# Hybrid short-conv and conformer block: tiles 3 and 4 of the FFN's input turned by VectorE and DRAM instead of TensorE

## The chip, the cores and the metric

The kernel runs on one core of one Trainium2 chip. The metric is device time in microseconds of one launch; of the kernel before three runs are shown. Besides, one execution was taken by the hardware profiler; views of that trace are quoted in fences. Engines are named as the profile names them: PE is TensorE (PEld its weight loads), DVE VectorE, ACT ScalarE, POOL GpSimd, SP SyncE, which here only issues DMAs (SPq). L659 is line 659 of the kernel.

## What is computed

One decoder block over 1024 tokens of width 1024, in float32, with 16 learned tokens ahead that are dropped at the end:

```
mix = mixer(rms_norm(h, pre_mix_norm), ...)       # input projection, two gated convolution groups, w_out
h   = h + rms_norm(mix, post_mix_norm)
xn  = rms_norm(h, pre_ffn_norm)
ff  = (silu(xn @ w_gate) * (xn @ w_up)) @ w_down
out = h + rms_norm(ff, post_ffn_norm)
```

The change lies between the mixer's output projection and the first gate and up products. There, token-major rows of `h` are normalised (`xn`) and have to be turned, so that the model dimension lies on partitions and they can be the moving operand of the gate and up products.

## The kernel before

**Precision.** Every product runs as three float32r matmuls, high x high, high x low and low x high (`mm3`, L105 to 109). For every operand ScalarE makes the high part (a cast) and VectorE the low part (a subtraction).

**Output projection in product groups.** The 1024 tokens are eight tiles of 128. `group` (L858) computes the output projection of three, three and two tiles: (0, 1, 2), (3, 4, 5), (6, 7). In a group the loop runs over the eight blocks k of the contraction; before each of the first six k the function given for that step in `at` is traced, and `at[6]` ahead of the last two. Everything stands under a manual schedule, so each engine, and each engine's DMA queue, runs its instructions in the order in which this Python code issues them. At the end of a group `leave_psum` (L617) empties the PSUM banks: ScalarE squares, VectorE multiplies by the gain gB_post.

**Norms.** `norms` (L633) takes a group's tiles: it forms the first inverse root, adds the residual rows (`hs`, loaded by `residual_x`, L628), writes `h` to DRAM (hd), squares, forms the second inverse root, and scales with gB_ffn into the tiles hn0 to hn7 (L651). `between` and `first` are pieces of other work traced inside it.

**Turning.** There are two ways. `turn` (L654) gives a tile to TensorE: eight 128x128 transposes into two PSUM banks, which ScalarE copies to the raw blocks (and, for tile 3, also casts and VectorE subtracts for B11). The other way takes tiles 0, 1 and 2: `send` (L668) lets VectorE transpose 32x32 blocks (STREAM_TRANSPOSE) and writes the tile to DRAM (xd); `fetch` (L672) reads it back with four DMAs so that the blocks come to their places; `receive` (L677) casts and copies into the raw blocks and B11. All of these DMAs, the weight loads and the residual rows go through SP's queue.

**Blocks.** raw[q, b] holds half q of the model dimension for tiles 4b to 4b+3. B11 is raw[0, 0] as high and low parts, B21 is raw[1, 0]. The gate and up products run in pairs of weight blocks by a Strassen-like scheme with seven products each (`Pair`, L723); the first two products, of pairs 0 and 1, read B11, all four tiles of it. The next two read B21, and T2 (sums of raw blocks, `t1_sum`, `t2_sum`, L915 to 930) comes after them.

**Where the pieces stood.** Group (6, 7) had tile 3's turn ahead of its sixth k (`b21`, L972, with B21's casts), and the turns of tiles 4 and 5, B11's last parts for T1 and the first operands ahead of its last two k (`early`, L978). Tiles 3, 4 and 5 were normalised before the group's code began.

**Buffers.** Two pools matter. `wp` has three buffers for each of the tags ws, wh, wl (raw weights, high and low parts). `tp` has five buffers of one tag, "t", and takes the two gains gB_post and gB_ffn (until the norms of the last group), the tiles hn, and some of the gate and up weights:

```
tp = ctx.enter_context(tc.tile_pool(name="tp", bufs=5))                              # L64
n[i] = row(tp, "t", f"hn{i}", TT)[:, :D]                                             # L644, in norms
if i == 1 or ((m, j % 2) == (0, 0) if j > 1 else (m, j) == (1, 1)):                  # L736, in Pair.load
    t = row(tp, "t", f"u{j}{m}{i}", TT)[:, :D]
else:
    t = wp.tile([P, D], F32, tag="ws", name=f"u{j}{m}{i}")
```

A buffer is given to a new tile when all that read or write the old one, by the program, have done so; the first instruction that writes the new tile waits for that. The pool `rp`, four buffers of 8 KB a partition, holds half of the projection's moving data and, as those are used up, B21; the transposed tiles on their way to DRAM go there after the change.

Of the kernel before, what the change touches and what calls it, by code (L numbers as in the profile page):

```python
# [8 lines left out]
F32 = mybir.dt.float32  # L9
# [45 lines left out]
def hybrid_block(ctx: ExitStack, tc: tile.TileContext, xT, x, w_first, w_in, w_out, w_gate, w_up, w_down, par, g_post, g_ffn, g_out, out):  # L55
# [39 lines left out]
    def big(name, dt=F32R, pool=None):  # L95

        return (pool or xg).tile([P, 4 * HALF], dt, tag="x", name=name)
# [56 lines left out]
        nc.sync.dma_start(raw_w["o", k], w_out[k])  # L154

    def split_o(k, eng=None):
        if k in (3, 4):
            wu[k] = [held[k - 3][:, q, :] for q in range(2)]
        else:
            wu[k] = [wp.tile([P, D], F32R, tag=t, name=f"{t}_o{k}") for t in ("wh", "wl")]  # L160
        nc.scalar.copy(wu[k][0], raw_w["o", k])
        (eng or nc.vector).tensor_tensor(wu[k][1], raw_w["o", k], wu[k][0].bitcast(F32), op=ALU.subtract)

    def third(j):
# [463 lines left out]
    def residual_x(i):  # L628
        h = hp.tile([P, D], F32, tag="h", name=f"h{i}")
        nc.sync.dma_start(h, x[i * P : (i + 1) * P, :])  # L630
        return h

    def norms(grp, left, s1, hs, between=None, first=None):  # L633
        n_ = len(grp)
        v = sm.tile([P, 16], F32, tag="s2", name=f"pm{grp[0]}")
        nc.vector.tensor_tensor(v[:, :n_], s1[:, 0:n_], s1[:, 4 : 4 + n_], op=ALU.add)
        r = rsqrt_n(v[:, :n_], 1.0 / D, RMS_EPS, n_, f"pm{grp[0]}")
        if first:
            first()
        v2 = sm.tile([P, 16], F32, tag="s2", name=f"pf{grp[0]}")  # L640
        n = {}
        for q, i in enumerate(grp):
            nc.vector.scalar_tensor_tensor(hs[i], left[i], r[:, q : q + 1], hs[i], op0=ALU.mult, op1=ALU.add)
            n[i] = row(tp, "t", f"hn{i}", TT)[:, :D]  # L644
            nc.scalar.activation(n[i], hs[i], AF.Square, accum_out=v2[:, q : q + 1])
            nc.sync.dma_start(hd[i], hs[i])
        if between:
            between()
        r = rsqrt_n(v2[:, :n_], 1.0 / D, RMS_EPS, n_, f"pf{grp[0]}")
        for q, i in enumerate(grp):  # L650
            nc.vector.scalar_tensor_tensor(n[i], hs[i], r[:, q : q + 1], gB["ffn"], op0=ALU.mult, op1=ALU.mult)  # L651
        return n

    def turn(i, n, at=(0, 1)):  # L654
        c = slice((i % 4) * P, (i % 4 + 1) * P)
        for q in range(2):
            pt = bank(at[q], f"pt{i}_{q}")
            for k in range(4):
                nc.tensor.transpose(pt[:, k * P : (k + 1) * P], n[:, (4 * q + k) * P : (4 * q + k + 1) * P], ident)  # L659
            p4 = pt.rearrange("p (a b) -> p a b", a=4)  # L660
            nc.scalar.copy(raw[q, i // 4][:, :, c], p4)
            if (q, i // 4) == (0, 0):
                nc.scalar.copy(B11[0][:, :, c], p4)
                nc.vector.tensor_tensor(B11[1][:, :, c], p4, B11[0][:, :, c].bitcast(F32), op=ALU.subtract)

    xd = {i: dram.tile([P, D], F32, tag=f"xd{i}", name=f"xd{i}") for i in range(3)}

    def send(i, n, t):  # L668
        nc.vector.transpose(t.rearrange("p (j k q) -> p j k q", j=4, k=8), n.rearrange("p (k j q) -> p j k q", k=8, j=4))
        nc.sync.dma_start(xd[i], t)  # L670

    def fetch(i, n):  # L672
        for j in range(4):
            src = xd[i].rearrange("(i r) (j x) -> j r i x", i=4, j=4)[j]
            nc.sync.dma_start(n[32 * j : 32 * j + 32].rearrange("r (i x) -> r i x", i=4), src)

    def receive(i, n):  # L677
        c = slice(i * P, (i + 1) * P)
        split4 = lambda t: t[:, :, c].rearrange("p k (i q) -> p k i q", i=4)
        for q in range(2):  # L680
            n4 = n.rearrange("p (i k q) -> p k i q", i=4, k=8)[:, 4 * q : 4 * q + 4]
            if q == 0:
                nc.scalar.copy(split4(B11[0]), n4)
                nc.vector.tensor_tensor(split4(B11[1]), n4, split4(B11[0]).bitcast(F32), op=ALU.subtract)
            nc.scalar.copy(split4(raw[q, 0]), n4)

    st = None
    free = [5, 6, 7, 4, 0, 1, 2, 3]
# [34 lines left out]
    class Pair:  # L723
# [19 lines left out]
        def a_side(self, n, m):  # L743
            a11, a12 = self.u[m, 0][:, :512], self.u[m, 0][:, 512:]
            if n not in (1, 2):
                a21, a22 = self.u[m, 1][:, :512], self.u[m, 1][:, 512:]
            if n == 1:
                s = a11
            elif n == 6:
                add(a21, a21, a22)  # L750
                sub(a11, a21, a11)
                s = a11
            elif n == 2:
                s = a12
            elif n == 5:
                s = a21
            elif n == 7:
                sub(a21, a22, a11)
                s = a21
            elif n == 3:  # L760
                sub(a12, a12, a11)
                s = a12
            else:
                s = a22
            return s
# [92 lines left out]
    def group(grp, ks, at):  # L858
        pm = {i: [bank(b, f"po{i}{q}") for q, b in enumerate(OUT_BANKS[j])] for j, i in enumerate(grp)}

        def mm(i, k):
            c = slice(i * P, (i + 1) * P)
            for q in range(2):
                d = slice(q * 512, (q + 1) * 512)
                mm3(pm[i][q], yh[k][:, c], yl[k][:, c], wu[k][0][:, d], wu[k][1][:, d], k == ks[0], k == ks[-1])

        for s, k in enumerate(ks[:-2]):
            at.get(s, lambda: None)()
            for i in grp:
                mm(i, k)  # L870
        at.get(6, lambda: None)()
        for i in grp:
            for k in ks[-2:]:
                mm(i, k)
        s1 = sm.tile([P, 16], F32, tag="s1", name=f"s1_{grp[0]}")
        return s1, {i: leave_psum(i, pm[i], s1, q) for q, i in enumerate(grp)}

    def ahead(k=None, n=None):

        def f():  # L880
            if k is not None:
                split_o(k)
            if n is not None:
                load_o(n)

        return f
# [13 lines left out]
        fetch(i, hn[i])  # L900

    def turns(*grp, at=(0, 1)):
        return lambda: [turn(i, hn.pop(i), at if q else (0, 1)) for q, i in enumerate(grp)]

    def back(i):
        return lambda: receive(i, hn.pop(i))

    hs = {i: residual_x(i) for i in (3, 4, 5)}
    s1, left = group((3, 4, 5), middle, {1: ahead(0, 5), 2: ahead(1, 6), 3: lambda: [ahead(2, 7)(), back(0)()], 4: back(1), 5: back(2)})
    hn = norms((3, 4, 5), left, s1, hs)  # L910

    n_hi = [0]
    X = {1: B11}

    def t1_sum(i):  # L915
        c = slice(i * P, (i + 1) * P)
        r11, r12 = raw[0, 0], raw[0, 1]
        sub(r11[:, :, c], r12[:, :, c], r11[:, :, c])
# [13 lines left out]
    def split_lo(o, src):  # L932
        for h in range(2):
            s = slice(2 * h, 2 * h + 2)
            sub(o[1][:, s, :], src[:, s, :], o[0][:, s, :].bitcast(F32))
# [4 lines left out]
    def copy_hi(o, src):  # L940
        for h in range(2):
            s = slice(2 * h, 2 * h + 2)
            nc.scalar.copy(o[0][:, s, :], src[:, s, :])
# [6 lines left out]
    def a_high(s, *places):  # L950
        if s >= len(order) or s in made:
            return
        j, n = order[s]
        if j > 1 and n == 1 and j + 1 < NP:
            pairs[j + 1] = Pair(j + 1)
        src = sums.pop(s, None) or [pairs[j].a_side(n, m) for m in range(2)]
        made[s] = [operand_hi(src[m], f"{n}_{j}{m}", places[m] if places else None) for m in range(2)]
        high[s] = src
# [6 lines left out]
        a_high(s, *places)  # L965
        a_low(s)

    def pairs_load():
        split_o(7)
        pairs[1].load(0, (0,))  # L970

    def b21():  # L972
        turns(3)()
        X[2] = pair("B21", (rp, rp))
        copy_hi(X[2], raw[1, 0])
        split_lo(X[2], raw[1, 0])

    def early():  # L978
        for q in range(2):
            raw[q, 1] = blocks(big(f"raw{q}1", F32))  # L980
        turns(4, 5, at=(5, 6))()
        pairs[1].load(0, (1,))
        for i in range(2):
            t1_sum(i)
        a_side(0)
        a_side(1, (hp, "h"), (jp, "jk"))

    hs = {i: residual_x(i) for i in (6, 7)}
    s1, left = group((6, 7), up, {1: ahead(5), 2: lambda: [split_o(6), pairs[0].load(0)], 3: pairs_load, 5: b21, 6: early})
    r11, r21, r12, r22 = raw[0, 0], raw[1, 0], raw[0, 1], raw[1, 1]  # L990
    T2r = blocks(big("T2r", F32))
    results = {s: pairs[order[s][0]].product(order[s][1], made.pop(s)) for s in range(2)}
# [2 lines left out]
        pairs[0].load(1)  # L995
        a_low(2)

    hn = norms((6, 7), left, s1, hs, between, lambda: a_high(2))
    results.pop(0)()
    del left, hs  # L1000
    table(AF.Silu)
# [3 lines left out]
    st = ctx.enter_context(tc.tile_pool(name="st", bufs=11, reuse_waits="tile"))  # L1005
    X[6] = pair("T2", (rq, None))
    a_side(3)
    for f in (t2_sum, t2_hi, t2_lo):
        for i in range(2):
            f(i)  # L1010

# [380 lines left out]
```

## Time and profile before

| | us |
|---|---|
| median of 3 runs | 964.51 |
| lowest, highest | 964.1, 964.77 |
| the profiled execution | 964.41 |
| its span, first to last instruction | 962.6 |

| engine | busy us | share of the span |
|---|---|---|
| PE | 954.8 | 99% |
| PEld | 821.6 | 85% |
| DVE | 711.5 | 74% |
| ACT | 406.7 | 42% |
| POOL | 249.7 | 26% |

In the rows of a timeline the first number is the start in us from the span's start, the second the length; then engine, line, operation, output <- inputs, shapes and the number of instructions merged. A bracket tells how long the engine was idle before and what ended it. In the rows of waits stand who waited, for whom, and the total us, the number of times and the longest. Matmuls overlap: one of 512 columns is shown as 0.39 us long, and they start 0.227 us apart. The window of this change is 300 to 345 us of the span: group (6, 7) and the first gate products.

### The profile page before, as it was taken

The page shows a single profiled execution, that of the slowest core. Times are in us where ns is not written, and L with a number is a line of the kernel's source. Part 1 is how long each engine was busy: PE and PEld are TensorE (multiplying, and loading weights), DVE is VectorE, ACT ScalarE, POOL GpSimd, SP SyncE. Part 2 cuts the span into 40 slices and gives each one's busy share as a digit, 9 for nine tenths or more (in the row PEclk, how much of TensorE's full clock was granted, in tenths as well). Part 3 has the DMA queues.
Part 4 walks back from the last instruction along what each step waited for, and adds up shares of the span by engine and source line. Part 5 has one row for each costly group of instructions (what it writes and reads, how often), then busy time and mean ns, then how long its engine had stood idle before and what let it go on. Part 6 is the DMA issues. An engine that isn't in the chain of part 4 may idle for free.

```text
span 962.6 us, 12503 instructions
## 1 busy us (share of the span) xinstructions
PE 954.8 (99%) x4570; PEld 821.6 (85%) x4570; DVE 711.5 (74%) x1028; ACT 406.7 (42%) x666; POOL 249.7 (26%) x219
## 2 busy tenths in 40 slices
PE   9999999999999999999999999999999999999997
PEld 9999999998888888888888888888888888888885
DVE  7699999886476999997766866877776543546775
ACT  8533423365546754454343443343442333322341
POOL 1277954552000000003124124132141111111210
PEclk9999999999999999999999999999999999999999
DMA  8011211214347510564433533623419899856866
GB/s 312 23 45 46 65 45 45 66 44 151 134 152 252 189 64 29 190 259 168 164 153 118 211 132 110 239 108 135 154 49 371 285 350 372 256 176 211 317 209 245
DMA packets 60877, 159.82 MB, mean 166 GB/s; under 512 B 6416, under 2 KB 8976, under 8 KB 60816
## 3 DMA queue, kind: packets, MB, share of 16 engines
q1 hardware_dynamic: 44352, 106.98, 30.8%
q0 software_dynamic: 11088, 40.38, 13.0%
q10 hardware_dynamic: 5376, 11.67, 3.4%
q8 instruction: 36, 0.59, 0.2%
q14 instruction: 25, 0.20, 0.1%
HBM read 108.67 MB, written 50.33 MB: 165 GB/s over the span
## 4 chain that ended last, share of the span: by engine, by line
PE 99%; DVE 0%; issue 0%; DVEq 0%; ACT 0%
PE x L107 8%; PE x L109 8%; PE x L108 8%; PE y L107 6%; PE y L109 6%; PE y L108 6%; PE qx L109 4%; PE qx L108 4%; PE qx L107 4%; PE qy L108 3%; PE qy L109 3%; PE qy L107 3%; PE po L107 3%; PE po L109 3%; PE po L108 3%; PE p_v L108 2%
## 5 line engine op out<-in xcount | busy, mean ns | idle before, releaser
L710 ACT CAST op<-u 128x512 fp32r<-128x512 f32 x154 | 93.6, 622 | 180.1 <-DVE u L697 92.8
L697 DVE TENSOR_TENSOR op<-u,op 128x512 fp32r<-128x512 f32 x154 | 118.1, 807 | 41.3 <-ACT op L710 41.3
L697 DVE TENSOR_TENSOR db<-wb,db 128x512 fp32r<-128x512 f32 x77 | 54.9, 716 | 85.2 <-ACT db L1197 84.9
L700 POOL TENSOR_TENSOR C<-C,C 128x512 f32<-128x512 f32 x9 | 15.5, 1723 | 361.8 <-DMA gdA<-U 199.2
L1197 ACT CAST db<-wb 128x512 fp32r<-128x512 f32 x77 | 47.2, 620 | 117.8 <-PE qx L109 55.6
L107 PE MATMUL qx<-db,a 128*128 128x512 f32 x176 | 68.5, 389 | 0.0
L108 PE MATMUL qx<-db,a 128*128 128x512 f32 x176 | 68.5, 389 | 0.0
L109 PE MATMUL qx<-db,a 128*128 128x512 f32 x176 | 68.5, 389 | 0.0
L694 DVE TENSOR_TENSOR U<-y,U 128x512 f32<-128x512 f32 x66 | 43.1, 682 | 18.2 <-PE y L109 18.2
L108 PE MATMUL qy<-db,a 128*128 128x512 f32 x132 | 51.5, 390 | 0.0
L107 PE MATMUL qy<-db,a 128*128 128x512 f32 x132 | 51.4, 389 | 0.0
L109 PE MATMUL qy<-db,a 128*128 128x512 f32 x132 | 51.4, 389 | 0.0
L1070 POOL DMA_DIRECT2D a<-gdS x44 | 23.2, 528 | 91.7 <-PE qx L109 46.0
L700 POOL TENSOR_TENSOR U<-U,U 128x512 f32<-128x512 f32 x17 | 28.2, 1659 | 60.2 <-ACT U L825 46.5
L382 DVE SCALAR_TENSOR_TENSOR ac<-g,pr,ac 128x512 f32<-128x512 f32 x56 | 42.0, 750 | 0.0
L382 DVE SCALAR_TENSOR_TENSOR ae<-d,pr,ae 128x512 f32<-128x512 f32 x56 | 42.0, 749 | 0.0
L108 PEld LDWEIGHTS qx<-db,a 128*128 128x128 f32 x176 | 33.0, 188 | 6.9
L107 PEld LDWEIGHTS qx<-db,a 128*128 128x128 f32 x176 | 33.0, 188 | 6.9
L109 PEld LDWEIGHTS qx<-db,a 128*128 128x128 f32 x176 | 33.0, 188 | 6.8
L107 PE MATMUL x<-B21h,op 128*128 128x512 f32 x88 | 34.3, 390 | 0.0
L109 PE MATMUL x<-B21h,op 128*128 128x512 f32 x88 | 34.2, 389 | 0.0
L108 PE MATMUL x<-B21l,op 128*128 128x512 f32 x88 | 34.2, 389 | 0.0
(359 smaller groups left out, 2912.9 us busy)
## 6 DMA issues: line engine op xcount, KB each, us to landing
a<-gdS POOLq DMA_DIRECT2D x44, 512.0 KB, 4.7
a<-gdA POOLq DMA_DIRECT2D x33, 512.0 KB, 5.7
u<-w_gate_u SPq DMA_DIRECT2D x22, 512.0 KB, 5.2
u<-w_up_u SPq DMA_DIRECT2D x22, 512.0 KB, 5.9
gdS<-HI SPq DMA_DIRECT2D x44, 256.0 KB, 2.5
gdA<-HI SPq DMA_DIRECT2D x33, 256.0 KB, 2.0
gdS<-GS SPq DMA_DIRECT2D x33, 256.0 KB, 2.7
ws_o<-w_out_u SPq DMA_DIRECT2D x14, 512.0 KB, 5.2
```

The costliest lines, as they stand in the source:

```text
L107: nc.tensor.matmul(o, lh, rh, start=start, stop=False, skip_group_check=again)
L108: nc.tensor.matmul(o, lh, rl, start=False, stop=False, skip_group_check=again)
L109: nc.tensor.matmul(o, ll, rh, start=False, stop=stop, skip_group_check=again)
L382: nc.vector.scalar_tensor_tensor(out if i == n - 1 else acc, src[:, i : i + HALF], w(i), init if i == first else acc, op0=ALU.mult, op1=AL ...
L694: (eng or nc.vector).tensor_tensor(o, a, b, op=ALU.add)
L697: (eng or nc.vector).tensor_tensor(o, a, b, op=ALU.subtract)
L700: (eng or nc.vector).tensor_tensor(o, a, b, op=ALU.mult)
L710: nc.scalar.copy(t[:, 0, :], src)
L1070: nc.gpsimd.dma_start(loads[n, j], gd[an][j])
L1197: nc.scalar.copy(t[:, 0, :], b)
```

## The change

- `norms` of tiles 3, 4 and 5 is no longer traced ahead of group (6, 7) but at its step 1 (`step1`), with the pieces of step 1 inside; with `parts=True` it returns the three last multiplications, the first of which is traced there and the other two in `step2`.
- Tiles 3 and 4 go by `send`, `fetch` and `receive`: tile 3 is sent in step 1, fetched in step 2 and received in `early`; tile 4 is sent in step 3, fetched in `early` and received inside the norms of group (6, 7). Only tile 5 is turned by TensorE there, in banks 5 and 6.
- The split of weight 5 is parted in high (ScalarE) and low (VectorE), and the loads of the gate and up weights and of the residual rows of tiles 6 and 7 are spread over steps 1 to 3.
- B21 is cast for tiles 0 to 2 in step 4 and for tile 3 in `early`; `t1_sum` for tiles 0 and 1 moves behind the norms of group (6, 7).

```diff
     def split_o(k, eng=None):
+        split_o_hi(k)
+        split_o_lo(k, eng)
...
-    def norms(grp, left, s1, hs, between=None, first=None):
+    def norms(grp, left, s1, hs, between=None, first=None, parts=False):
...
-        for q, i in enumerate(grp):
-            nc.vector.scalar_tensor_tensor(n[i], hs[i], r[:, q : q + 1], gB["ffn"], op0=ALU.mult, op1=ALU.mult)
+        last = [lambda q=q, i=i: nc.vector.scalar_tensor_tensor(n[i], hs[i], r[:, q : q + 1], gB["ffn"], op0=ALU.mult, op1=ALU.mult) for q, i in enumerate(grp)]
+        if parts:
+            return n, last
+        for f in last:
+            f()
         return n
...
             nc.scalar.copy(raw[q, i // 4][:, :, c], p4)
-            if (q, i // 4) == (0, 0):
-                nc.scalar.copy(B11[0][:, :, c], p4)
-                nc.vector.tensor_tensor(B11[1][:, :, c], p4, B11[0][:, :, c].bitcast(F32), op=ALU.subtract)
...
     def receive(i, n):
-        c = slice(i * P, (i + 1) * P)
+        c = slice((i % 4) * P, (i % 4 + 1) * P)
...
-            if q == 0:
+            if q == 0 and i < 4:
                 nc.scalar.copy(split4(B11[0]), n4)
                 nc.vector.tensor_tensor(split4(B11[1]), n4, split4(B11[0]).bitcast(F32), op=ALU.subtract)
-            nc.scalar.copy(split4(raw[q, 0]), n4)
+            nc.scalar.copy(split4(raw[q, i // 4]), n4)
...
-    hn = norms((3, 4, 5), left, s1, hs)
-
...
-    def pairs_load():
+    def turned(i):
+        send(i, hn[i], big(f"xt{i}", F32, rp)[:, :D])
+
+    def between_5():
+        split_o_lo(5)
+        pairs[0].load(0, (0,))
+
+    def step1():
+        n, muls = norms((3, 4, 5), left, s1, hs, between_5, lambda: split_o_hi(5), True)
+        hn.update(n)
+        pairs[1].load(0, (1,))
+        muls[0]()
+        turned(3)
+        hn_muls.extend(muls[1:])
+
+    def step2():
+        split_o(6)
+        pairs[0].load(0, (1,))
+        fetch(3, hn[3])
+        for f in hn_muls:
+            f()
+
+    def step3():
         split_o(7)
         pairs[1].load(0, (0,))
-
-    def b21():
-        turns(3)()
+        turned(4)
+        for i in (6, 7):
+            hs[i] = residual_x(i)
+
+    def step4():
         X[2] = pair("B21", (rp, rp))
-        copy_hi(X[2], raw[1, 0])
-        split_lo(X[2], raw[1, 0])
+        b21_hi(slice(0, 3 * P))
+
+    def b21_hi(c):
+        nc.scalar.copy(X[2][0][:, :, c], raw[1, 0][:, :, c])
+
+    def b21_lo(c):
+        sub(X[2][1][:, :, c], raw[1, 0][:, :, c], X[2][0][:, :, c].bitcast(F32))
 
     def early():
         for q in range(2):
             raw[q, 1] = blocks(big(f"raw{q}1", F32))
-        turns(4, 5, at=(5, 6))()
-        pairs[1].load(0, (1,))
-        for i in range(2):
-            t1_sum(i)
         a_side(0)
+        b21_lo(slice(0, 3 * P))
+        back(3)()
+        b21_hi(slice(3 * P, 4 * P))
+        b21_lo(slice(3 * P, 4 * P))
+        turns(5, at=(5, 6))()
+        fetch(4, hn[4])
         a_side(1, (hp, "h"), (jp, "jk"))
 
-    hs = {i: residual_x(i) for i in (6, 7)}
-    s1, left = group((6, 7), up, {1: ahead(5), 2: lambda: [split_o(6), pairs[0].load(0)], 3: pairs_load, 5: b21, 6: early})
+    hn_muls = []
+    s1, left = group((6, 7), up, {1: step1, 2: step2, 3: step3, 4: step4, 6: early})
...
+    def first():
+        a_high(2)
+        back(4)()
+
+    hn.update(norms((6, 7), left, s1, hs, between, first))
...
-    for f in (t2_sum, t2_hi, t2_lo):
+    for f in (t1_sum, t2_sum, t2_hi, t2_lo):
         for i in range(2):
             f(i)
```

More of the change, by code (lines that the diff above doesn't have):

```diff
@@ L156, in split_o, with split_o_hi @@
     def split_o(k, eng=None):
+        split_o_hi(k)
+        split_o_lo(k, eng)
+    def split_o_hi(k):
         if k in (3, 4):
@@ L161, in split_o, with split_o_lo @@
         nc.scalar.copy(wu[k][0], raw_w["o", k])
+    def split_o_lo(k, eng=None):
         (eng or nc.vector).tensor_tensor(wu[k][1], raw_w["o", k], wu[k][0].bitcast(F32), op=ALU.subtract)
@@ L661, in turn @@
             nc.scalar.copy(raw[q, i // 4][:, :, c], p4)
-            if (q, i // 4) == (0, 0):
-                nc.scalar.copy(B11[0][:, :, c], p4)
-                nc.vector.tensor_tensor(B11[1][:, :, c], p4, B11[0][:, :, c].bitcast(F32), op=ALU.subtract)
-    xd = {i: dram.tile([P, D], F32, tag=f"xd{i}", name=f"xd{i}") for i in range(3)}
+    xd = {i: dram.tile([P, D], F32, tag=f"xd{i}", name=f"xd{i}") for i in range(5)}
     def send(i, n, t):
@@ L902, in turns @@
     def turns(*grp, at=(0, 1)):
-        return lambda: [turn(i, hn.pop(i), at if q else (0, 1)) for q, i in enumerate(grp)]
+        return lambda: [turn(i, hn.pop(i), at if q or len(grp) == 1 else (0, 1)) for q, i in enumerate(grp)]
     def back(i):
@@ L996, in between @@
         a_low(2)
-    hn = norms((6, 7), left, s1, hs, between, lambda: a_high(2))
+    def first():
+        a_high(2)
+        back(4)()
+    hn.update(norms((6, 7), left, s1, hs, between, first))
     results.pop(0)()
```

## The prediction

> **What bounds the kernel.** I read the page's busy shares and its chain first. They say where a microsecond counts.
>
> ```profile
> span 962.6 us, 12503 instructions
> ...
> PE 954.8 (99%) x4570; PEld 821.6 (85%) x4570; DVE 711.5 (74%) x1028; ACT 406.7 (42%) x666; POOL 249.7 (26%) x219
> ...
> PE 99%; DVE 0%; issue 0%; DVEq 0%; ACT 0%
> ```
>
> TensorE is busy for 99% of the span and is 99% of the chain that ends last. So an instruction taken from TensorE comes off the time, and a wait put into TensorE's stream is added to it. Everything else counts only if it makes TensorE wait. The profiled execution took 964.41 us, 1.81 more than its span, and lies 0.10 under the median of 964.51. The sum below is made against 964.41. About 0.2% (1.9 us) is what a measurement of this kernel can tell from no change.
>
> Next I read the timeline of TensorE across the third product group (tokens of tiles 6 and 7), where tiles 3, 4 and 5 are turned.
>
> ```profile
> 300.91 0.39 PE L107 MATMUL po<-wh_o,y 128*128 128x512 f32 x1
> ...
> 314.51 1.03 PE L659 MATMUL pt<-ident,hn 128*128 128x128 f32 x8
> ...
> 318.14 1.91 PE L659 MATMUL pt<-ident,hn 128*128 128x128 f32 x16
> ...
> 325.35 0.39 PE L107 MATMUL x<-B11h,op 128*128 128x512 f32 x1
> ```
>
> The group starts at 300.91 and has gone through five of its k when tile 3 is turned at 314.51: 13.60 us, 2.72 per k. Tile 3's eight transposes and the sixth k fill 314.51 to 318.14, 3.63, so the transposes cost 0.91. Tiles 4 and 5 and the last two k fill 318.14 to 325.35, 7.21; less 5.44 that is 1.77, or 0.89 a tile. At 325.35 the first gate product begins with no gap.
>
> **What is removed.** The transposes of tiles 3 and 4 leave TensorE: 0.91 + 0.89 = 1.80 us. If nothing waits, the sixth k ends at 300.91 + 6 x 2.72 = 317.23, tile 5 is turned there, and the first gate product is due at 325.35 - 1.80 = 323.55. That is the whole gain, and the rest asks whether tile 3 is in B11 by 323.55, since this product reads all four tiles of B11.
>
> **What is added, and its queue.** Tile 3 now goes through the way of tiles 0 to 2: VectorE's transpose, a write to DRAM (xd), four reads back (fetch), casts. All DMAs of this stage are on SP's queue, which issues in order. So I read that queue, with the first three tiles' trip.
>
> ```profile
> 281.69 2.53 SPq L670 DMA_DIRECT2D xd<-jk  x3
> ...
> 316.53 0.33 SPq L740 DMA_DIRECT2D u<-w_gate_u  x1
> 316.91 0.42 SPq L740 DMA_DIRECT2D u<-w_up_u  x1
> ...
> 331.39 0.46 SPq L740 DMA_DIRECT2D u<-w_gate_u  x1
> 335.64 0.33 SPq L740 DMA_DIRECT2D u<-w_up_u  x1
> ```
>
> ```profile
> SPq L740 <- DVE hn L651: 3.7, 1, 3.7
> ```
>
> ```profile
> 280.37 3.49 DVE L669 STREAM_TRANSPOSE jk<-hn 128x1024 f32<-128x1024 f32 x3
> ...
> 309.42 3.68 DVE L651 SCALAR_TENSOR_TENSOR hn<-h,r_pf,gB_ffn 128x1024 f32<-128x1024 f32 x3
> 313.01 3.49 DVE L162 TENSOR_TENSOR wl_o<-ws_o,wh_o 128x1024 fp32r<-128x1024 f32 x3
> ...
> 333.13 2.48 DVE L651 SCALAR_TENSOR_TENSOR hn<-h,r_pf,gB_ffn 128x1024 f32<-128x1024 f32 x2
> ```
>
> The load at 335.64 is the point on which I decide. It is the second of two issued by one call (line 995). The first goes at 331.39; the second waits 3.7 us until VectorE has read gB_ffn for the last time (333.13 + 2.48 = 335.61). Tag "t" of pool tp has five buffers, and these loads can only take one that its last reader has left. So the pool is full there, and SP stands still meanwhile.
>
> Now count tag "t" in the changed step1. gB_post and gB_ffn are held until the end of the group and its norm. norms has just made hn3, hn4 and hn5. That is five. Then step1 calls pairs[1].load(0, (1,)), which for m = 1, j = 1 takes a sixth tile of the same tag. In the kernel before, the same load stands behind the turns of tiles 3, 4 and 5, which gave buffers back. In the changed order nothing has. hn3 is free only after its fetch and cast, hn4 later, the gains later still; hn5 is free when TensorE has turned tile 5. The first of them is hn5, at 317.23 + 1.03 = 318.26 (eight transposes, from the row at 314.51).
>
> Behind this load on SP are queued: the write of tile 3, the second weight load of pair 0, the four fetches of tile 3, a weight load of pair 1, the write of tile 4, the two residual rows of tiles 6 and 7, and the fetch of tile 4. Without the wait tile 3's write could go when VectorE has scaled (309.42 + 1.23) and transposed it (1.16 to 1.2), at 311.9. With it, the write goes one issue after 318.26, by the spacing of 316.53 and 316.91 at 318.64: 6.7 us late.
>
> **When tile 3 arrives.** ScalarE's timeline has the first trip's end.
>
> ```profile
> 291.34 0.62 ACT L683 CAST B11h<-hn 128x512 fp32r<-128x512 f32 x1 [9.58 <-DMA hn<-xd]
> 291.87 1.13 ACT L685 COPY raw<-hn 128x512 f32<-128x512 f32 x2
> ...
> 322.47 0.62 ACT L710 CAST op<-u 128x512 fp32r<-128x512 f32 x1 [0.61 <-DMA u<-w_gate_u]
> 323.75 0.62 ACT L710 CAST op<-u 128x512 fp32r<-128x512 f32 x1 [0.67 <-DMA u<-w_up_u]
> 324.28 0.59 ACT L622 ACTIVATE sq<-po 128x512 f32<-128x512 f32 x1
> ```
>
> From the first write's issue (281.69) to the first cast (291.34) the trip takes 9.65. Its shortest form comes from the landing rows of the writes, of the fetches and of the weight loads, in this order:
>
> ```profile
> DMA to landing us min/median/max: 2.6/2.7/3.1
> ```
>
> ```profile
> DMA to landing us min/median/max: 3.8/5.0/5.5
> ```
>
> ```profile
> DMA to landing us min/median/max: 3.5/4.5/6.8
> ```
>
> Shortest: 2.6, three more issues of 0.33 (as at 316.53), 3.8: 7.4. Longest: two loads issued 0.38 apart (316.53, 316.91) were ready 1.28 apart (322.47, 323.75), so a 512 KB transfer behind another waits for its bytes. Tile 3's write is behind a load (3.5, then 1.28, less 0.38: 4.4 in place of 2.6), and its fetches behind a second one (1.28): 9.65 + 1.8 + 1.28 = 12.7. I take 9.65, the one measured trip, whose own writes stood beside two others. Arrival: 318.64 + 9.65 = 328.29.
>
> Then ScalarE's order sets the product's start. The product writes banks 5 and 6, which tile 5's transposes fill and which ScalarE empties only after tile 3's three casts and copies (291.34 to 293.00, 1.66) and the cast of B21's last quarter (0.62): with the copy (0.59) 2.87 after arrival, 331.16. Against 323.55 TensorE stands idle for 7.6 us. Ends: 5.4 with the short trip, 10.7 with the long one.
>
> **The clock after the idle.** The trace of before has no idle of TensorE inside, so the price is bounded by the start.
>
> ```profile
> 1.06 3.67 PE L89 MATMUL warm<-ones 128*128 128x128 f32 x16 [1.06 <-DVE pr L113]
> ...
> 6.92 0.45 PE L281 MATMUL p_v<-xh,fl 128*128 128x348 f32 x1
> 7.20 0.32 PE L281 MATMUL p_g1a<-xh,fl 128*128 128x348 f32 x1
> 7.36 0.32 PE L107 MATMUL p_g<-xh,fh 128*128 128x348 f32 x1
> ```
>
> Matmuls of 348 columns start 0.28 apart up to 7.20 and 0.16 apart from there. So from 1.06 to 7.2 TensorE ran at about half its later rate, which loses 3.05 us. After 7.6 us of idle this is between nothing and 3.05; I take the middle, 1.5, since the idle is real but far shorter than the one ahead of a run. The Trainium skill, "TensorE: Matmul & The Clock Gate", the part on the HAM clock gate, says that TensorE goes to half its clock after an idle window and needs about 3.4 us of work to leave it; by that the loss would be an estimated 1.7 and the sum 0.2 higher. The trace agrees in kind (half rate at the start), but its slow stretch is 6.1 us.
>
> **Parts that I cost at nothing.** The norm's steps move behind one k and keep their rows; the low part of weight 5 (1.16) moves into VectorE's wait for the squares. If that cover were gone, tile 3 would be 1.2 later; the wait on SP is longer. The B21 casts by tiles, t1_sum put behind the norm of tiles 6 and 7, and tile 4's trip run while TensorE has 10.9 us of products of pairs 0 and 1 on B11 ahead; uncovered, the tile-wise casts would cost one more ScalarE access, 0.62. The dropped branch for tile 3 in turn takes a ScalarE cast away and receive puts it back.
>
> **Sum.** 964.41 - 1.80 + 7.6 + 1.5 = 971.7, and 971.8 on the median's side. Ends: 964.41 - 1.80 + 5.4 = 968.0, and 964.41 - 1.80 + 10.7 + 3.05 = 976.4.
>
> **Rivals.** *No wait at the sixth tile* (the loads pass each other, or a buffer is free that I count as held): the write goes at 311.9, tile 3 arrives at 321.55, and the product can start at 324.4, 0.87 late, or in time with the short trip. That gives 962.6 to 963.6, not slower, and it decides wherever tile 3's write is issued before about 311. For it: the schedule then fits almost to the microsecond. Against it: the wait at 335.64 on the same tag. *A second wait behind the first*: tile 4's copies stand on ScalarE ahead of the squares of tiles 6 and 7. From the group's squares (324.28) to the second scaled tile (335.61) took 11.3. After tile 3's arrival stand the 2.87, a copy and two casts (1.7) and these 11.3, so hn7 comes 15.9 after it, and TensorE turns it 2.87 + 3 x 5.44 = 19.2 after: 3.3 of slack. The copies stand 4.5 into the 11.3, at 9. If tile 4 lands later than 9 + 3.3 after tile 3, each further microsecond is TensorE's; 2 to 4 of them give 974 to 976. SP's order (four issues, a landing and a fetch later) puts it at 6 to 8, which speaks against.
>
> **Chances.** Wait at the sixth tile, as summed: 0.80. No such wait: 0.13, nearly all within 0.2%, since even 1.80 is under 1.9. Second wait too: 0.07, slower as well. So faster 0.04, same 0.10, slower 0.86. The range 967.0 to 976.5 takes the bounds of the first case, a microsecond below them, and most of the third; the second lies outside.
>
> **What would show it.** Right: on SP's queue a gap of some 9 us between the first two gate-weight loads, ended by tile 5's transposes, and the write of tile 3 right behind it near 318.6; TensorE idle before the first gate product, ended by ScalarE's copy out of tile 5's bank; 24 transposes in place of 40; matmuls up to twice as far apart just after the gap. Wrong: tile 3's write near 312 and no gap on TensorE, with 962.6 to 963.6. A gap with the clock unchanged would put only the 1.5 wrong.

## The result and the profile after

| | before | after |
|---|---|---|
| median, us | 964.16 (5 runs) | 972.79 (5 runs) |
| lowest, highest | 963.85, 964.77 | 972.21, 973.22 |
| the profiled execution, us | 964.41 | 972.49 |
| its span | 962.6 | 970.7 |

The ratio is 1.0089, with a 95% interval of 1.0078 to 1.0100: slower by 8.6 us, where 971.8 was forecast. The page of the changed kernel first. Its second row gives busy time of the engines, its third the granted clock of TensorE in 40 slices of 24 us.

```profile
span 970.7 us, 12488 instructions
...
PE 955.0 (98%) x4554; PEld 821.1 (85%) x4554; DVE 713.6 (74%) x1030; ACT 406.5 (42%) x666; POOL 249.6 (26%) x219
...
PEclk9999999999999799999999999999999999999999
...
PE 98%; DMA 1%; ACT 0%; DVE 0%; SPq 0%; issue 0%; DVEq 0%; ACTq 0%
```

TensorE has 16 matmuls fewer, the transposes of two tiles, and yet its busy time has not fallen, 955.0 after 954.8. The chain of work that ended last now has 1% of DMA in it, where it had none. And one slice in the whole run has a lower clock: the fourteenth, 316 to 340 us. All of the loss lies in that slice. SP's queue shows how it begins:

```profile
308.12 0.33 SPq L746 DMA_DIRECT2D u<-w_gate_u  x1
317.61 0.33 SPq L746 DMA_DIRECT2D u<-w_up_u  x1
317.99 0.43 SPq L676 DMA_DIRECT2D xd<-xt  x1
318.51 0.38 SPq L746 DMA_DIRECT2D u<-w_up_u  x1
323.66 1.75 SPq L681 DMA_DIRECT2D hn<-xd  x4
```

SP issues nothing from 308.45 to 317.61. The load at 317.61 is the one that takes a sixth tile of tag "t". Two rows of SP's waits, taken over 300 to 345 us, say for what it stood:

```profile
SPq L746 <- DVE hn L656: 10.7, 2, 6.8
SPq L746 <- PE pt L668: 2.3, 1, 2.3
```

The longest wait of the first row, 6.8, lasts until VectorE has written hn5 (near 315.2), and the 2.3 of the second until TensorE has turned it. So the buffer that the load takes is hn5's. Right behind the load goes the write of tile 3 (xd<-xt), and 5.67 later the reads back. VectorE had tile 3 ready long before:

```profile
310.48 1.25 DVE L675 STREAM_TRANSPOSE xt<-hn 128x1024 f32<-128x1024 f32 x1
```

So the write could have gone at 311.7 and went 6.3 later. TensorE's timeline gives both ends of the wait:

```profile
300.22 0.39 PE L107 MATMUL po<-wh_o,y 128*128 128x512 f32 x1
...
316.54 1.04 PE L668 MATMUL pt<-ident,hn 128*128 128x128 f32 x8
...
322.64 0.39 PE L109 MATMUL po<-wh_o,ybl 128*128 128x512 f32 x1
331.02 0.80 PE L107 MATMUL x<-B11h,op 128*128 128x512 f32 x1 [7.99 <-ACT raw L670]
...
332.04 0.63 PE L109 MATMUL x<-B11h,op 128*128 128x512 f32 x1
332.46 0.63 PE L107 MATMUL x<-B11h,op 128*128 128x512 f32 x1
...
336.31 0.40 PE L107 MATMUL x<-B11h,op 128*128 128x512 f32 x1
336.54 0.39 PE L108 MATMUL x<-B11l,op 128*128 128x512 f32 x1
...
349.94 0.82 PE L668 MATMUL pt<-ident,hn 128*128 128x128 f32 x6
```

The transposes of tile 5 end at 316.54 + 1.04 = 317.58, and SP's load goes 0.03 later. The product group ends at 322.87, and the first gate product starts at 331.02, released by ScalarE's copy out of tile 5's bank (line 670). ScalarE's timeline has what stands between tile 3's arrival and that copy:

```profile
324.86 0.62 ACT L716 CAST op<-u 128x512 fp32r<-128x512 f32 x1 [7.50 <-DMA u<-w_up_u]
328.17 0.62 ACT L689 CAST B11h<-hn 128x512 fp32r<-128x512 f32 x1 [2.70 <-DMA hn<-xd]
328.70 1.13 ACT L691 COPY raw<-hn 128x512 f32<-128x512 f32 x2
329.86 0.62 ACT L1006 CAST B21h<-raw 128x512 fp32r<-128x512 f32 x1
330.39 1.06 ACT L670 COPY raw<-pt 128x512 f32<-128x512 f32 x2
```

The first row is a second transfer that was late. It is the second weight load of pair 0, which stood behind the stop too (issued at 318.51). ScalarE works in the order of the code, and this cast stands ahead of tile 3's. Tile 3 came last, 2.70 after ScalarE was free again, and so sets the time. But tile 3 alone on time would not have saved all: its casts could then start at about 325.5, and the product, 2.85 later, at about 328.3. By this estimate from the rows some 5.5 of the 8.2 would have stayed. What stopped SP made both late.

After the idle time the matmuls are 0.43 apart up to 336.31, then 0.23. Busy time by stretch says it with the clock (the column behind POOL's):

```profile
322.00:331.00 9.00, 1.03 (x5) 0.53 (x3) 3.54 (x4) 3.41 (x7) 0.00 (x0) 0.73 0.81 254
331.00:337.00 6.00, 5.98 (x15) 4.71 (x16) 4.90 (x13) 5.02 (x14) 0.00 (x0) 0.56 0.73 247
337.00:343.00 6.00, 6.00 (x28) 4.97 (x27) 5.43 (x10) 5.64 (x11) 0.00 (x0) 1.00 0.70 259
```

In 6 us there are 15 matmuls at a clock of 0.56, against 28 at 1.00. Both stretches read as fully busy. That is why TensorE's busy time did not fall: slow matmuls count as work, and this part of the loss stands in the page only as a digit of the clock.

**The sum from the traces.** In this execution group (6, 7) starts 0.69 earlier than in the one of before (300.22, 300.91), which belongs to the work ahead of it. The transposes bring 1.80: the group lasts 22.65 in place of 24.44. The product starts at 331.02 instead of 322.86, 8.16 late (the 7.99 in the bracket counts from the end of the last matmul, which is shown longer than its step). From it to the turn of tiles 6 and 7 go 18.92, where before had 16.33 (325.35 to 341.68): 2.59 for the clock. So -0.69 - 1.80 + 8.16 + 2.59 = 8.26, against 8.1 of span.

### The profile page after: what moved, and what is told of

Read it like the earlier page. It is cut to its first block, busy times and chain, and to the rows that moved or that the text cites. A ratio compares the mean times of both kernels' runs of the same rounds, so it can differ in the third digit from the quotient of the medians.

```text
span 970.7 us, 12488 instructions
## 1 busy us (share of the span) xinstructions
PE 955.0 (98%) x4554; PEld 821.1 (85%) x4554; DVE 713.6 (74%) x1030; ACT 406.5 (42%) x666; POOL 249.6 (26%) x219
## 4 chain that ended last, share of the span: by engine, by line
PE 98%; DMA 1%; ACT 0%; DVE 0%; SPq 0%; issue 0%; DVEq 0%; ACTq 0%
PE x L107 8%; PE x L109 8%; PE x L108 8%; PE y L107 6%; PE y L109 6%; PE y L108 6%; PE qx L109 4%; PE qx L108 4%; PE qx L107 4%; PE qy L108 3%; PE qy L109 3%; PE qy L107 3%; PE po L107 3%; PE po L109 3%; PE po L108 3%; PE p_v L108 2%
## 5 line engine op out<-in xcount | busy, mean ns | idle before, releaser
L107 PE MATMUL x<-B11h,op 128*128 128x512 f32 x88 | 35.4, 402 | 8.0 <-ACT raw L670 8.0
L108 PE MATMUL x<-B11l,op 128*128 128x512 f32 x88 | 35.2, 400 | 0.0
L109 PE MATMUL x<-B11h,op 128*128 128x512 f32 x88 | 35.2, 400 | 0.0
```

What stands on the lines that cost most here:

```text
L107: nc.tensor.matmul(o, lh, rh, start=start, stop=False, skip_group_check=again)
L108: nc.tensor.matmul(o, lh, rl, start=False, stop=False, skip_group_check=again)
L109: nc.tensor.matmul(o, ll, rh, start=False, stop=stop, skip_group_check=again)
```

## Experiments

The theory: the load that takes a sixth tile of a five-buffer tag stops SP, tile 3's write stands behind it, and everything else follows. Its rivals: tile 3's long way through DRAM, or something else that the change moves, is to blame, or a weight load that comes too late. Each ratio is to runs of the kernel before on the same chip, whose medians were 963.93 to 964.20. No kernel leaves out work; one adds some.

**The load out of the way.** In step1 the line `pairs[1].load(0, (1,))` is dropped, and the load comes back in `early`, behind the turn of tile 5:

```diff
-        pairs[1].load(0, (1,))
...
         turns(5, at=(5, 6))()
+        pairs[1].load(0, (1,))
         fetch(4, hn[4])
```

> The changed kernel with one load moved: the weight load of pair 1 that takes the sixth tile of tag t goes from step 1 to behind tile 5's turn. Theory (the wait on SP for a sixth buffer is the whole loss): tile 3's write goes near 311.8, it arrives near 319 to 321, no idle of TensorE before the first gate product or under 1 us, no slow matmuls; 1.8 us less than before, 962.4 (961.9 to 963.4). Rival A (the trip through DRAM is too long in itself, or the DMAs added collide): TensorE still idles several us, 966 or more. Rival B (the loss lies in ScalarE's or VectorE's new order): the same 972.8.

966.54 (965.63 to 968.56), ratio 1.0026 (1.0017 to 1.0035). Tile 3's write goes at 311.30, its reads at 314.08, and the first product starts at 323.42 after 0.48 of idle: 7.5 of the 8.0 are gone, so the load at its place in step1 was the cause, and tile 3's way through DRAM is short enough. Yet 4.1 of the expected gain did not come. Another wait has appeared, on ScalarE and then on TensorE (two views):

```profile
328.12 0.62 ACT L716 CAST op<-u 128x512 fp32r<-128x512 f32 x1 [3.75 <-DMA u<-w_up_u]
```

```profile
331.32 0.50 PE L107 MATMUL x<-B11h,op 128*128 128x512 f32 x1 [2.16 <-DVE jk L629]
```

Now the load is last in the queue. It is issued at 319.16, behind a weight load of pair 1, tile 4's write and two residual rows, and ScalarE waits 3.75 for it. Behind this cast on ScalarE stand the squares of tiles 6 and 7; they and VectorE's multiplications (line 629) empty the banks that the second product needs, and TensorE waits 2.16. The expectation had taken the load as free to move; it has a due time at both ends.

**Two places between.** The same load, put behind tile 3's write in step1, and in another kernel behind tile 3's reads in step2:

```diff
-        pairs[1].load(0, (1,))
         muls[0]()
         turned(3)
+        pairs[1].load(0, (1,))
```

> The same load traced behind tile 3's write, still ahead of its fetch. Theory (what counts is which transfers stand behind the wait): the write lands near 314.4, the fetch still waits for tile 5's turn and goes near 318.4 behind two weight loads; arrival near 324.5, product near 327.4 in place of 322.9: 4.5 us of idle, 1.8 gained, and between 0 and 2.6 for the clock: 966.9 to 969.5. Rival (SP's standing still costs by its length, whatever is behind it): as the changed kernel, 972.8.

969.88 (969.53 to 970.35), ratio 1.0059 (1.0045 to 1.0073): a small miss, 0.4 above the range, and clear of the rival's 972.8.

```profile
312.20 0.32 SPq L676 DMA_DIRECT2D xd<-xt  x1
318.21 0.81 SPq L746 DMA_DIRECT2D u<-w_up_u  x2
319.11 1.80 SPq L681 DMA_DIRECT2D hn<-xd  x4
```

```profile
PE x L107 <- ACT raw L670: 5.1, 1, 5.1
```

The write is early, SP still stands until 318.21, and now only the reads are behind the wait. TensorE's idle time falls from 8.0 to 5.1, where 4.5 was expected, and the clock still falls.

```diff
-        pairs[1].load(0, (1,))
...
         fetch(3, hn[3])
+        pairs[1].load(0, (1,))
         for f in hn_muls:
```

> The same load traced behind tile 3's fetch. SP stands still from about 315 to 317.6 as before, but only a weight load of pair 1, tile 4's write and the residual rows are behind it. Theory: arrival near 319 to 321, no idle, 962.4 (961.9 to 963.4). Rival (any wait of SP here costs): 964 or more.

963.38 (962.9 to 965.18), ratio 0.9995 (0.9986 to 1.0004).

```profile
312.02 0.32 SPq L676 DMA_DIRECT2D xd<-xt  x1
...
314.83 1.75 SPq L681 DMA_DIRECT2D hn<-xd  x4
318.24 0.35 SPq L746 DMA_DIRECT2D u<-w_up_u  x1
```

SP again waits for tile 5's turn, until 318.24, but nothing of tile 3 is behind it. 972.79, 969.88, 963.38: with each step of tile 3 that passes ahead of the load, time comes back, and with both the whole loss. Of the 1.80 that the transposes are worth only 0.8 arrives. In its profile the first product starts 0.25 late (323.76 after a group that ends at 323.51), still by the copy out of tile 5's bank, and the matmuls that read T2 wait 0.2 for ScalarE; the rest of the missing microsecond is in smaller gaps.

**The wait by itself.** Does a stop of SP cost anything when nothing urgent is behind it? In the kernel before, the load is moved out of `early` and ahead of the residual rows, where the buffer isn't free either:

```diff
-        pairs[1].load(0, (1,))
...
+    pairs[1].load(0, (1,))
     hs = {i: residual_x(i) for i in (6, 7)}
```

> The kernel before, with the same weight load traced ahead of the residual rows of tiles 6 and 7, so that on SP it waits for a sixth buffer until TensorE has turned tile 3, near 315.6, and five loads stand behind it. Theory (a wait of SP costs only by what is late behind it, and here all five land before ScalarE needs them or within a microsecond): 964.2 (963.9 to 965.2). Rival (a wait of SP for a buffer costs by its own length, some 4.8 us): 967 or more.

964.77 (964.51 to 965.42), ratio 1.0007 (0.9998 to 1.0015).

```profile
306.26 1.52 SPq L646 DMA_DIRECT2D hd<-h  x2
315.78 0.33 SPq L740 DMA_DIRECT2D u<-w_up_u  x1
316.22 0.87 SPq L630 DMA_DIRECT2D h<-x_tok  x2
```

SP stands for 8 us here too, from 307.78 to 315.78 (tile 3's turn by TensorE, 314.67 and 1.03 long, gives the buffer), and with weights and residual rows behind it the median stays within 0.1%. The length of the stop isn't the price; what is behind it is.

**The buffer or the order?** SP's order stays as in the changed kernel, but tile 3's reads go to the free half of its own turning buffer, so that hn3 gives back a "t" buffer as soon as VectorE has turned it:

```diff
-        send(i, hn[i], big(f"xt{i}", F32, rp)[:, :D])
+        xt = big(f"xt{i}", F32, rp)
+        send(i, hn[i], xt[:, :D])
+        if i == 3:
+            hn[i] = xt[:, D:]
```

> The changed kernel with SP's order untouched, but tile 3 is read back from DRAM into the unused half of the tile that it was transposed into, so that hn3's buffer is free as soon as VectorE has transposed it (near 311.7) and not after tile 5's turn. Theory (the buffer, not the place of the load in the order, holds SP): the load goes near 311.8, tile 3's write right behind it near 312.2 and landing behind the load's bytes near 316.5, arrival 321 to 322.5, product at 323 to 325.4, with 0 to 2.5 of idle and up to 1.8 for the clock: 962.5 to 966.7. Rival (the order alone decides): 972.8.

965.64 (964.38 to 966.55), ratio 1.0015 (1.0006 to 1.0024).

```profile
312.01 0.33 SPq L746 DMA_DIRECT2D u<-w_up_u  x1
312.39 0.42 SPq L676 DMA_DIRECT2D xd<-xt  x1
...
318.02 2.58 SPq L681 DMA_DIRECT2D xt<-xd  x4
```

```profile
325.90 0.50 PE L107 MATMUL x<-B11h,op 128*128 128x512 f32 x1 [2.23 <-ACT raw L670]
```

The load now goes at 312.01 instead of 317.61, at the same place in the order: what held it there was the full tag. 7 of the 8.6 us are back. What is left is the load ahead of the write, and the clock behind the idle time: the reads wait for the write's landing until 318.02, 5.63 after its issue, where the kernel with the load behind the reads had 2.81 (312.02 to 314.83). The profiled execution took 966.55, the slowest of ten.

**The clock by itself.** TensorE gets 36 matmuls to do while it waits. Their results go to a bank that nothing reads:

```diff
+    idle = bank(0, "idle")
+    for _ in range(36):
+        nc.tensor.matmul(idle, ones, wu[7][0][:, :512], start=True, stop=True)
     results = {s: pairs[order[s][0]].product(order[s][1], made.pop(s)) for s in range(2)}
```

> The changed kernel with 36 dummy matmuls of 512 columns (8.2 us, into a bank that nobody reads) ahead of the first gate product, where TensorE idles 8.1 us. They add work and leave nothing out. Theory (the clock falls because TensorE idles): the first product's twelve matmuls run 0.23 apart in place of 0.43, 2.6 us less: 970.2 (969.7 to 971). Rival (the matmuls are slow for another reason, the DMAs or the casts beside them): 972.8 as it is.

971.55 (971.34 to 971.8), ratio 1.0075 (1.006 to 1.0091): better than without the matmuls, but 0.55 above the range expected.

```profile
332.73 0.50 PE L107 MATMUL x<-B11h,op 128*128 128x512 f32 x1 [0.83 <-ACT raw L670]
...
333.54 0.40 PE L107 MATMUL x<-B11h,op 128*128 128x512 f32 x1
```

Three matmuls in 0.81 at once, where the changed kernel needs 1.44 (331.02 to 332.46). From the first gate product to the turn of tiles 6 and 7 go 16.46 in place of 18.92: the slow matmuls were the clock's, and the clock's fall came from the idle time. The median gained only 1.24 of these 2.46. In the profile tile 3 arrives later: from its first read's issue to B11's cast it takes 5.78 (324.10 to 329.88), where the changed kernel took 4.51. Counted from the group's start (300.70), the product comes 1.2 later than there, and that is the missing gain in this execution. Why the reads take longer is open.

**Tile 5's banks.** In the changed kernel the product waits for ScalarE to empty banks 5 and 6, not for B11. Tile 5 is turned in banks 0 and 1 instead:

```diff
-        turns(5, at=(5, 6))()
+        turns(5)()
```

> The changed kernel with tile 5 turned in banks 0 and 1, and nothing else. Theory (after tile 3 arrives, ScalarE's copies and casts up to the copy out of bank 5 are on the path): the first gate product starts with B11's low part, near 329.5 in place of 331.0: 971.3 (970.9 to 971.8). Rival (the product waits for B11 alone): 972.8 as it is.

971.49 (970.58 to 972.14), ratio 1.0076 (1.0062 to 1.009). The wait is 6.5 and names B11's cast:

```profile
PE x L107 <- ACT B11h L689: 6.5, 1, 6.5
```

So ScalarE's work from that cast to the copy is on the path, and the rest of the wait is tile 3's arrival. Its price is known only roughly. The medians differ by 1.3 (972.79 less 971.49), but two of the four executions took 970.6 and 970.9 and two 972.1. In the profiled one, 970.87, the product follows B11's cast by 0.67 (328.93 to 329.60) in place of 2.85, the cast itself comes 0.7 later after the group's start, and the slow matmuls cost 2.1 in place of 2.6.

**A better version.** The load behind tile 3's reads, tile 5 in banks 0 and 1, and `t1_sum(1)` back in `early`:

```diff
-        pairs[1].load(0, (1,))
...
         fetch(3, hn[3])
+        pairs[1].load(0, (1,))
...
-        turns(5, at=(5, 6))()
+        turns(5)()
+        t1_sum(1)
...
-    for f in (t1_sum, t2_sum, t2_hi, t2_lo):
+    t1_sum(0)
+    for f in (t2_sum, t2_hi, t2_lo):
```

> The kernel with the load behind tile 3's fetch, and two more edits: tile 5 is turned in banks 0 and 1 instead of 5 and 6, which the first product needs, and t1_sum of tile 5 goes back into the group. Theory (of the 1.8 us only 0.8 came through because the first gate product waited 0.36 for the copy out of bank 5 and product 4 of pair 0 waited 0.48 for T2): both waits go, 962.5 (962.2 to 963.0), 1.7 under the kernel before. Rival (the missing microsecond lies elsewhere): as without the two edits, 963.4.

963.11 (962.77 to 964.26) against 964.12, ratio 0.9990 (0.9981 to 0.9999): the lowest median here, 1.0 us under the kernel before. The expected 962.5, at most 963.0, is missed, and the interval overlaps that of the kernel without the two edits (0.9986 to 1.0004), so what they bring is not shown. The first product starts with no gap. The profile is of the slowest of eleven executions, 964.26, and has one wait left, at the third product (two views):

```profile
331.72 1.14 ACT L691 COPY raw<-hn 128x512 f32<-128x512 f32 x2 [1.20 <-DMA hn<-xd]
```

```profile
335.81 0.50 PE L107 MATMUL x<-B21h,op 128*128 128x512 f32 x1 [1.02 <-ACT U L803]
```

ScalarE stands 1.20 for tile 4's reads; behind that copy are the squares of the last norm and the copies that empty the first product's banks. Whether an execution near the median has this wait too is not shown; 963.11 is 1.15 less, about its length. Tile 4 was then moved to behind the first product's results:

```diff
     def first():
         a_high(2)
-        back(4)()
...
     results.pop(0)()
+    back(4)()
```

> The kernel with the load behind the fetch, banks 0 and 1 and t1_sum of tile 5 in the group, and besides tile 4's two copies on ScalarE moved from ahead of the squares of tiles 6 and 7 to behind the first gate product's copies. Theory (what is left is ScalarE waiting for tile 4's fetch, with the squares and the copies out of the first product's banks behind it, so that the third product waits up to 1.2 us): that wait goes, 962.4 (961.9 to 962.9), 1.8 under the kernel before. Rival (the rest is not there): as without the move, 963.1. One cost is open: tile 4's buffer of tag t is then held longer, and the first load of pair 0's second half takes it.

963.55 (963.14 to 964.94) against 963.93, ratio 0.9998 (0.9989 to 1.0007). A miss. The profiled execution took 963.19. In it the third product is on time: tiles 6 and 7 are turned at 339.32, 39.0 after the group's start, where before had 40.8. The cost that was left open came: SP waits 2.9 for ScalarE's copy of tile 4 before it can issue the next load, though ScalarE doesn't wait for that load's bytes. And later matmuls wait instead:

```profile
PE x L107 <- ACT U L803: 0.5, 1, 0.5
PE y L784 <- ACT T2h L930: 0.2, 1, 0.2
```

This execution is 0.7 under the median of before (963.93). These two waits make 0.7 of the 1.1 that it misses of the 1.8; the rest I have not located.

## Why the prediction was right

**Transposes, -1.80.** Right: the group is 22.65 long, 1.79 less, with 24 transposes in all.

**The wait at the sixth tile.** Right in place and cause. Forecast was the load at 318.26, measured 317.61, which is 318.30 on the clock of before's execution (0.69 added). The place of the load, and the buffer by itself, each undo it.

**Trip of tile 3, 9.65.** 10.18 (317.99 to 328.17), and put together otherwise. The write took 5.6 to land. The row of landing times of the writes of tiles 3 and 4 (line 676) has it as the shorter of two:

```profile
DMA to landing us min/median/max: 5.6/5.9/6.3
```

The forecast's long end gave it 4.4 behind a load. From the write's issue to the reads' went 5.67, and 4.51 from there to the cast. In the first three tiles' trip the same two parts were 2.63 (281.69 to 284.32) and 7.02 (284.32 to 291.34): a fast write, and reads that were slow among twelve. So the whole, 9.65, came near by luck: two differences of 3.0 and 2.5 went against each other.

**ScalarE behind it, 2.87.** 2.85.

**Idle, 7.6.** 8.16, through the trip.

**The clock, 1.5.** 2.59: the term that was mis-sized. The middle between nothing and the start's 3.05 was taken because the idle was short, with no row that has such an idle time; what was measured lies near the upper end. The 36 extra matmuls brought back 2.46 of it. The Trainium skill, "TensorE: Matmul & The Clock Gate", the part on the HAM clock gate, gave an estimated 1.7 by about 3.4 us at half rate. Here the slow stretch was 5.3 (331.02 to 336.31), so for this idle time the page's figure is short.

**The sum, 971.7.** 972.49 profiled. Idle +0.56 and clock +1.09, less the 0.69 by which the group began early, make +0.96; with 0.16 less in the rest of the run, this is the 0.8 by which the forecast fell short.

**Rival, no wait.** The kernel with the load behind the reads is this case: 963.38, inside 962.6 to 963.6. Its point, "wherever tile 3's write is issued before about 311", was not tried, but the time of the issue alone doesn't decide: with the write at 312.02 and nothing ahead of it the product is 0.25 late, with the write at 312.39 behind a load 2.4.

**Rival, second wait.** Not in the changed kernel: tile 4's copies start at 337.44, 9.3 after tile 3's cast, where the forecast had 6 to 8 and slack up to 12.3. With the first wait gone it is seen in one execution, for 1.0 us: tile 4's copies stand ahead of the squares on ScalarE, as described, but TensorE meets them at the third product and not at tile 7's turn.

**Parts at nothing.** The tile-wise casts and `t1_sum` behind the norm can't be told apart in the changed kernel, where the long wait covers them. In the kernels without it, waits of 0.2 to 1.0 stand at U's and T2's copies, and up to 1.0 of the 1.80 doesn't arrive. The forecast had no term for this, and which of the parts costs it is not shown. It had none for the weight load that ScalarE casts ahead of tile 3 either; tile 3 came later still, so nothing of it reached the sum.

## What to carry to other kernels

When an instruction that takes a buffer moves, count the tag's live tiles at its new place: on an in-order queue a full tag stops everything behind, and it costs what the most urgent transfer there costs, not the length of the stop. Moving the load later only helps up to its own due time; the best place was right behind the urgent transfers. And a wait put into TensorE, which is 99% busy here, was charged twice where it was 2.2 us or longer, as idle time and as slow clock behind it, and once where it was 1.0 or less. Nothing between was measured.

## What the runs showed that was not expected

**The clock falls after 2.2 us of idle.** After 8.0 and 5.1 of idle the matmuls were slow from the first, for 5.3 and 5.2, costing 2.6 and 2.5. After 6.5 (tile 5 in banks 0 and 1) they were slow for 3.9 only, costing 2.1, so the price doesn't simply grow with the idle time. After 2.16 (the load last) and 2.23 (the buffer sooner) the first three or four ran at full rate and the next ones 0.43 apart, for 3.4, costing 1.7. After 0.83 and 1.02 the clock stayed. Each of these is one execution. Rows of the case of 2.16, with the load last:

```profile
331.32 0.50 PE L107 MATMUL x<-B11h,op 128*128 128x512 f32 x1 [2.16 <-DVE jk L629]
...
332.25 0.63 PE L107 MATMUL x<-B11h,op 128*128 128x512 f32 x1
332.68 0.63 PE L108 MATMUL x<-B11l,op 128*128 128x512 f32 x1
...
335.24 0.45 PE L108 MATMUL x<-B11l,op 128*128 128x512 f32 x1
```

The Trainium skill, "TensorE: Matmul & The Clock Gate", the part on the HAM clock gate, states a window of about 3.4 us that runs on its own, and half the clock after an idle window. The stretches of 3.4 agree; that a whole idle window is needed does not, since 2.2 sufficed. A window that was mostly idle would explain the late start, but that is argued and was not tried.

**A write behind a load.** The 512 KB write of tile 3 needed 2.8 until its reads could go with nothing just ahead of it on the queue, and 5.6 behind a load of the same size issued 0.4 earlier. The Trainium skill, "DMA: Bandwidth & Descriptors", the part on queues, rings and completion order, says that each DMA engine takes a queue's descriptors in ring order, which agrees.
